# Adding pairs of gated squares on VectorE ahead of the channel sums in a hybrid SSD and latent attention layer, with a new issue order

## The chip, the cores and the metric

The kernel runs on one core of a Trainium2 chip. The metric is the device time of one execution in microseconds. The kernel before takes 652.14 us, the median of 3 runs (651.75 to 652.39).

A core has a matrix engine (TensorE, PE), a vector engine (VectorE, DVE), an activation engine (ScalarE, ACT), a general one (GpSimd, POOL) and a queue engine that here only starts transfers (SyncE, SP). Each runs its own list of instructions in order and waits for the others by semaphores. SBUF is the on-chip memory, 128 partitions wide; PSUM holds what PE accumulates.

## The reference

One layer of an encoder, for 512 new frames and 64 frames of a running stream (576 tokens, width 1024). The input is normalised and projected once; half of the result goes through a state space scan (SSD), half through latent attention (MLA); both are concatenated, projected back, and a SwiGLU feed-forward layer follows.

```
h = rmsnorm(x, norm_mix);  proj = h @ w_in
xbc, conv_new = causal_conv(xbc, ...)                 # silu(conv), width 4
y, h_new = ssd_scan(xh, dt, A, B, C, h0)              # chunks
y = y + d_skip * xh
y = y * silu(z)                                       # the gate
y_ssd = rmsnorm(y, ssd_norm)                          # over 512 channels
... q, k, v; scores; softmax; values -> o
x = x + concat([y_ssd, o]) @ w_out
x = x + (silu(hf @ w_gate) * (hf @ w_up)) @ w_down,   hf = rmsnorm(x)
```

The change is in the sums that the norm of y_ssd needs: for each token, the sum of the squares of the 512 gated channels.

## The kernel before

Everything is kept with channels on partitions and tokens along the free dimension. A row of 1024 channels is 8 tiles of 128 x 576, 512 channels are 4 such tiles. Weights are split in a high and a low part (ACT line 112 copies the high part, DVE line 113 subtracts it), and most products are three PE passes over these parts, in two halves of 288 tokens.

The stages follow each other roughly like this. Up to 20 us: x and the first weights are loaded, and `ps_first` (line 128) makes the latent and query projections; sums of squares go through `ps_norm` (line 162), a product with a matrix of ones that both sums over partitions and copies the sum to all of them. 20 to 90 us: eight `conv_tile` steps (line 376), each a product `ps_in`, its evacuation to `up` (lines 383 to 385, DVE), one tap on ACT (line 390), three on DVE (line 392, tile `cacc`), a tanh on ACT (line 394). Among them stand the rope of the keys (line 301) and the step sizes of the scan (`dt`, `sp_a`, lines 339 to 354). 90 to 155 us: the scan in chunks of 128 tokens (0 to 3) and one of 64 (chunk 4, the running stream), by five steps: `chunk_a` (line 465; transposes `ps_x`, `ps_b`), `chunk_e` (line 501; decays E, products xw and E on DVE, lines 512 and 517), `chunk_b` (line 525; `ps_y`, skip at line 535, `ps_i`, lines 542 and 543), `chunk_s` (line 545; state product `ps_s`, states `h_c`, lines 557 and 558; h_0 is copied by ACT at line 554), and `gate` (line 565). The gate factors sz come from `z_tile` (lines 456 to 460).

`gate(c)` multiplies the chunk by sz (line 570, DVE, in place in xsd), squares it (line 572, ACT, tile ysq), sums the squares over the 512 channels by four products with ones, one for each 128 channels, into the bank ps_g (line 575), and copies the sum to its tokens of a row (line 576, ACT). `norm_y` turns this row into 1/rms, Ry (lines 171 to 178), `cat_tile` multiplies xsd by gain and Ry (line 752, four times) and splits it (lines 142 and 144) into `cat_y0` to `cat_y3`.

From about 145 us attention runs beside that: scores `sc` (line 660, and 666 for the stream), row maxima on DVE (line 643), exponentials on ACT (line 644), scaling (lines 645 to 650), transposes `ptp` (lines 682 and 690), values `pv`. `ps_o` (line 446) multiplies cat_y and the attention output by w_out, and DVE adds it to x (line 738). From about 225 us to the end the feed-forward layer runs (lines 855 and 956).

In what order an engine issues its work is written out by hand: `ISSUE` holds for each of the engines PE, DVE, ACT, POOL and SP a list of instruction numbers, in the order of emission, and `issue_in_order` binds each to the one before it in the list. Numbers that no list names are placed by the framework's scheduler. The steps are emitted in the orders `ORDER_CONV`, `ORDER_SSD`, `ORDER_ATT` and `ORDER_FFN`, which are the same in both kernels.

Of the kernel before, what the change touches and what calls it, by code (L numbers as in the profile page):

```python
# [14 lines left out]
ALU = mybir.AluOpType  # L15
# [39 lines left out]
def hybrid_layer_kernel(ctx: ExitStack, tc: tile.TileContext, a, o):  # L55
    nc = tc.nc
    pe, act, dve, pool, sp = nc.tensor, nc.scalar, nc.vector, nc.gpsimd, nc.sync
# [22 lines left out]
    def tmp(name, w=T):  # L80
        return tpool.tile([P, UPW], F32, tag="t", name=name)[:, :w]
# [10 lines left out]
    ones = cst.tile([P, P], F32, name="ones")  # L92
# [343 lines left out]
    def bank(tag, name):  # L436
        return (psq if tag == "sc" else psh).tile([P, 512], F32, tag=tag, name=name, bufs={"sc": 3, "pp": 3, "hm": 2}[tag])
# [128 lines left out]
    def gate(c):  # L566
        L = P if c < 4 else TS
        tk = slice(c * P, c * P + L)
        yv = xsd[:, :, tk]
        dve.tensor_tensor(yv, yv, sz[:, :, tk], ALU.mult)  # L570
        q = tmp(f"ysq{c}", 4 * L).rearrange("p (t l) -> p t l", t=4)
        act.activation(q, yv, AF.Square)
        ps = bank("pp", f"ps_g{c}")[:, :L]
        for t in range(4):
            pe.matmul(ps, ones, q[:, t], start=t == 0, stop=t == 3)
        act.copy(ssy[:, tk], ps)


# [456 lines left out]
    ps = [lbank(tag, f"ps_l0_{t}", 0) for t, tag in enumerate(("hm", "hm", "sc", "pp"))]  # L1035
# [112 lines left out]

ISSUE = {
    "PE": """  # L1150
0-7 20 14-15 8-10 21-25 11 16-19 32-43 56 12-13 26-31 44-49 62 50-55 68-73 57-61 74-79 92 63-67 80-85 98-100 93-97 110
86-91 104-109 122-127 142-143 134-135 101-103 116-121 136-141 144-147 111-115 128-133 148-171 174 270-274 175 222-229
176-179 172-173 180-221 230-269 275-370 373-420 371 421-468 372 469-590 613-636 591-612 637 641-644 638-640 657-660
665-712 661-664 713-736 645-656 737-760 763-766 771-818 767-770 761-762 819-826 859-861 833-836 862-864 837-840
827-828 831 865 829-830 866-867 832 868-870 880-883 841 845-852 871-873 853-856 842-844 874-879 884-887 857-858
904-909 888-891 910-912 892-900 925-926 913-915 901-903 927-934 916-921 935 939-940 922 936-938 923-924 949-951 964
952-963 965 941 966 945-948 967-970 942-944 971-979 987 980-983 988 984-986 989 991-993 1003 1015-1019 1004-1014
1020-1026 1029-1034 1043-1045 990 994-995 997-1002 1046-1048 996 1049-1054 1027 1035-1042 1028 1059-1064 1075-1076
1055-1056 1081-1092 1057 1077-1080 1058 1093-1104 1065 1121-1123 1066-1067 1071-1072 1068 1105 1124-1127 1069-1070
1128-1132 1108-1110 1073-1074 1133-1144 1106-1107 1119 1145-1156 1229-1237 1120 1238-1240 1111-1112 1115-1118  # L1160
1113-1114 1159-1161 1241-1252 1157 1253-1261 1158 1265-1268 1262-1264 1176 1269-1276 1177-1179 1162-1175 1277
1180-1183 1289 1278-1281 1290-1293 1184-1188 1282-1283 1189 1205-1206 1190-1195 1284-1287 1227 1196-1201 1288 1228
1202-1204 1207-1222 1294-1298 1223-1226 1299-1323 1342-1343 1348-1355 1344-1347 1324-1341 1356-1475 1572 1476-1504
1573 1575 1505-1511 1578 1581-1582 1512-1535 1584 1583 1536-1547 1579 1602 1548-1564 1580 1599-1600 1587-1589 1574
1593 1576 1565-1571 1585-1586 1605-1607 1626-1628 1577 1596 1608 1601 1620 1603-1604 1609-1610 1629 1590-1592
1611-1613 1621-1622 1647 1641 1594-1595 1614-1616 1635-1637 1623-1624 1632 1625 1648-1649 1644 1642-1643 1597-1598
1617-1619 1638 1633-1634 1653-1655 1639-1640 1656 1645-1646 1630 1658-1664 1631 1650-1652 1665-1669 1657 1682
1694-1703 1683-1689 1704-1705 1690-1693 1670-1681 1730-1736 1706-1717 1737-1741 1718-1729 1742-1763 1766 1764-1765
1778-1789 1767-1768 1790-1800 1769-1777 1802-1825 1850-1851 1801 1862-1873 1826-1849 1852-1861 1886-1909 1874-1885
1922-1934 1946-1957 1910-1921 1958-1969 1935-1945 1970-1989 2006-2013 1990-2005 2014-2034 2042-2053 2035-2041  # L1170
2054-2065 2078-2091 2093-2106 2066-2077 2107 2092 2108-2117 2123-2137 2118-2122 2138
""",
    "DVE": """
48 1 0 2-4 7 5-6 10 9 8 11-12 14 13 15-17 20 19 18 23 21-22 30 49 24-25 58 26-28 85 29 31-34 67 36 35 68 108 105 37
106 38 107 109 39 44 94 110 40 69 41 50-51 42 70 52 43 112 121 71 53 72 54 82 55 59-61 130 47 73 56 74 62 75 63 76 64
86-88 77-78 65 79 66 89-90 80 91 57 81 83 95-97 84 46 98-100 113-115 93 92 103 116-117 104 118 122 111 102 139 123 120
119 124 101 45 125-127 131-133 148 155 134-135 128 136 140-142 149 152 138 170 143 150 129 144 153 145 151 154 157 147
156 178 174 146 137 171 159-161 172 162 187 163 175 158 206 164 167 165 169 176 166 183 180 168 181 188 182 177 173
189 215 190 179 195 191-194 184 197 196 224 185-186 204 207 198-201 210 202 208 203 214 209 288 205 211 225 212-213
216-219 222 220 226-229 233 223 230 234 231-232 221 235-236 245 237 246 294 255 247-248 256 239 259 257 260 238  # L1180
263-264 258 261 240 262 241 267 265 242 266 270 243 271 244 268 249 274 251 269 253 250 252 254 275 278 289 277 290
276 272 295 279 287 286 280 282 307 273 297 283 317 291 281 298 296 299 284 318 292 302 285 316 293 319 306 309 303
300-301 312 310-311 313 326-327 304 362 308 328 322 305 320 363 367 323 329 364 321 330 324 336 331-332 325 337 314
366 315 340 333 365 341 377 334-335 344-345 338 346 352 347 339 348-349 342 350 353 351 359 358 343 360 354 356 361
355 357 370 368 371 369 372-373 376 375 374 390 382 378 384 379 383 385 389 386 380 397 387-388 381 405 393 391 395
394 403 392 420 396 401 398 402 462 400 404 406 399 408-409 407 410 463 416-417 464 411 418 412 414 421 469 419 422
413 423-425 428 426 415 427 431-432 438 429 433-435 430 436 439 437 440 442 441 443 466 444 465 446 451 467-468
452-453 455 454 473 447 445 474 470 475 477 448 476 456 472 457 478 449 458 480 482 479 471 488 490-492 481 489 450
493 503 485 504 487 459 505 495 494 507 506 460 500 508 496 486 461 497 518 520 510-511 483 502 521 509 560 522 515
484 519 517 540 523 543 558 524 538 498 526 537 501 512 527 516 513 563 525 528 514 530 499 529 532 542 565 547 555  # L1190
552 573 545 557 570 533 562 539 548 577 568 579 550 534 541 531 580 575 553 544 535 578 546
""",
    "ACT": """
0-5 8 6-7 11 10 9 12-16 18 17 21 20 24 19 23 22 40 25-27 44 51 28-31 50 32 55 33-35 37 36 48 59 41 49 63 38 42 39 67
43 45-47 52-54 56-57 71 58 60-62 64 75 65-66 76 68-70 91 72-74 93 78 89 79 84-85 82-83 80 102 86 88 81 87 100 115 98
96 77 90 103 97 95 99 92 101 125 104 155 109 108 94 111 114 112 110 113 106 116 107 162 141 121 105 117 139 138 118
126 123 134 127 136 119 135 137 120 133 140 128 142 122 129-130 151 144 148 124 209 131 146 132 153 143 147 145 150
149 154 157-158 152 156 159 211 160-161 163-164 169-171 165 167 172 179-180 168 185 173 186 174 188-189 175 166 191
176 192 177 187 178 181 194 193 190 199 195-196 182-184 198 207 200-201 212 214-215 226 202 216 218 208 204 217 233
197 205 210 213 219 203 232 220 206 222 225 227 239-240 228 223 241-243 270 221 230 224 229 236 234 271 235 237 277  # L1200
244 250 245 247 238 231 246 253 249 248 251 256 254 257-258 252 260 263 261-262 283 255 268 267 259 269 265 264 266
272-274 276 275 279-281 284 286 282 292 285 278 290 301 288 287 289 291 293-294 296 299 328-329 297 295 300 302-303
298 305 308 304 309 311 306-307 310 315 312-313 316 314 317 330 318 331 321 319-320 322-324 332 335 334 336 333 337
339 338 325 344 342 345-346 343 347-348 353 326 354 340 355 352 351 327 357 356 362 360 341 363-364 361 366 349 365
373 369 350 374 358 367 370 359 368
""",
    "POOL": """
0-3 7 18 28 4 8 5 9 6 10 26-27 11 29 12-17 20-22 19 23-25 31 30 32-42 53 55 57 59 54 56 58 60 43-52 61-73
""",
    "SP": """  # L1210
11-14 16 15 18 17 19-20 22 21 25 24 23 26 37 33 32 40-41 34 38 42-45 39 46-48 81 57 64 60 79 56 59 65 58 61-62 70 83
63 74 78 67-69 71-72 80 73 66 75 88-89 76-77 82 86 90 87 91-93 100 103 101-102 104-105
""",
}

# [98 lines left out]
```

## Time and profile before

| what | value |
|---|---|
| median of 3 runs | 652.14 us (651.75 to 652.39) |
| profiled execution, its own time | 652.35 us |
| its span | 650.6 us |
| granted TensorE clock | 1.00 |
| PE busy | 640.7 us, 98% |
| weight loads (PEld) busy | 613.4 us, 94% |
| DVE busy | 511.5 us, 79% |
| ACT busy | 338.3 us, 52% |
| POOL busy | 44.3 us, 7% |
| sums of the gate, line 575 | 40 records, 5.7 us of PE |

Busy times overlap, since the engines run beside each other. An fp32 product leaves two records on PE, so the twenty products of the gate are 40. Ends of matmuls are modelled, so PE can look busy where it waits; the weight loads (PEld) stand beside it as a second reading. In a list of waits each row names the waiting engine and tile, what released it, and the total, the number and the longest of the waits. In a timeline the bracket at the end of a row is the idle time ahead of it.

### The profile page before, as it was taken

What the parts mean: (1) busy time and instruction counts of PE and PEld (TensorE: products, weight loads), DVE (VectorE), ACT (ScalarE), POOL (GpSimd) and SP (SyncE); (2) the same over time, 40 slices, a digit from 0 to 9 for tenths busy, and PEclk for the clock granted to TensorE, in tenths of its full rate; (3) what the DMA queues carried; (4) which work ended last, traced back from release to release, by engine and by line L of the source; (5) the groups of instructions that cost most, each with busy time, mean ns of one, the idle gap of its engine ahead of it and who ended that gap; (6) DMA issues with size and microseconds to landing.
All of it is one profiled execution on the core that took longest, in us unless ns stands there. A gap on an engine that the chain in (4) does not pass through costs nothing.

```text
span 650.6 us, 11910 instructions
## 1 busy us (share of the span) xinstructions
PE 640.7 (98%) x4747; PEld 613.4 (94%) x4747; DVE 511.5 (79%) x932; ACT 338.3 (52%) x629; POOL 44.3 (7%) x79
## 2 busy tenths in 40 slices
PE   9999999998999999999999999999999999999996
PEld 9899999885897899999999999999999999999995
DVE  6998996799866699998996776866767776866555
ACT  7654345769676477564523545224533354335364
POOL 1330312001010000000000000000000000000022
PEclk9999999999999999999999999999999999999999
DMA  9620174315020222133322133212323223231004
GB/s 318 219 68 28 39 227 122 111 30 216 33 75 32 99 97 98 44 120 102 126 98 94 69 102 113 79 65 70 94 98 114 81 82 98 82 130 66 1 0 147
DMA packets 26151, 63.22 MB, mean 97 GB/s; under 512 B 3418, under 2 KB 10088, under 8 KB 25840
## 3 DMA queue, kind: packets, MB, share of 16 engines
q1 hardware_dynamic: 24560, 60.77, 27.7%
q0 software_dynamic: 816, 1.13, 0.8%
q8 instruction: 37, 0.61, 0.3%
q10 hardware_dynamic: 720, 0.57, 0.3%
q14 instruction: 18, 0.15, 0.1%
HBM read 58.03 MB, written 3.30 MB: 94 GB/s over the span
## 4 chain that ended last, share of the span: by engine, by line
PE 92%; DVE 4%; ACT 1%; issue 1%; POOL 1%; POOLq 0%; DVEq 0%; ACTq 0%
PE ps_x L855 21%; PE ps_d L956 18%; PE ps_z L855 10%; PE ps_o L446 8%; PE ps_in L128 7%; PE ps_y L855 5%; PE ps_z L446 4%; PE ps_l L956 3%; PE ps_first L128 2%; PE sc L660 2%; PE ps_p L855 2%; PE pv L707 1%; PE ptp L682 1%; PE ps_q L446 1%; PE ps_v L593 1%
## 5 line engine op out<-in xcount | busy, mean ns | idle before, releaser
L956 PE MATMUL ps_d<-pr,wh_d 128*128 128x288 f32 x576 | 115.4, 294 | 0.0
L855 PE MATMUL ps_x<-xop,wh_gu_S 128*128 128x288 f32 x504 | 102.0, 295 | 0.0
L956 PEld LDWEIGHTS ps_d<-pr,wh_d 128*128 128x128 f32 x576 | 92.5, 188 | 0.0
L956 PE MATMUL ps_d<-pr,wl_d 128*128 128x288 f32 x288 | 84.7, 295 | 0.0
L855 PEld LDWEIGHTS ps_x<-xop,wh_gu_S 128*128 128x128 f32 x504 | 80.9, 188 | 0.1
L855 PE MATMUL ps_x<-xop,wl_gu_S 128*128 128x288 f32 x252 | 74.2, 295 | 0.0
L112 ACT CAST wh_gu_S<-gu 128x1024 fp32r<-128x1024 f32 x44 | 46.2, 1050 | 37.4 <-PE ps_d L956 18.5
L113 DVE TENSOR_TENSOR wl_gu_S<-gu,wh_gu_S 128x1024 fp32r<-128x1024 f32 x44 | 53.6, 1222 | 8.3 <-PE ps_d L956 6.6
L956 PEld LDWEIGHTS ps_d<-pr,wl_d 128*128 128x128 f32 x288 | 54.0, 188 | 0.0
L112 ACT CAST wh_d<-wr_d 128x640 fp32r<-128x640 f32 (+1 forms) x32 | 21.5, 674 | 51.0 <-PE ps_x L855 20.4
L855 PEld LDWEIGHTS ps_x<-xop,wl_gu_S 128*128 128x128 f32 x252 | 47.2, 188 | 0.0
L128 PE MATMUL ps_in<-xs,wh_in 128*128 128x288 f32 x256 | 45.5, 299 | 1.0 <-DVE sp_a L351 1.0
L128 PEld LDWEIGHTS ps_in<-xs,wh_in 128*128 128x128 f32 x256 | 37.7, 189 | 1.5 <-ACT up L382 1.2
L855 PE MATMUL ps_z<-xop,gu_a 128*128 128x288 f32 x252 | 37.7, 294 | 0.0
L855 PE MATMUL ps_y<-xop,wh_gu_A 128*128 128x288 f32 x168 | 35.3, 295 | 0.0
L855 PE MATMUL ps_z<-xop,wh_gu_S 128*128 128x288 f32 x168 | 35.3, 297 | 0.0
L855 PEld LDWEIGHTS ps_z<-xop,gu_a 128*128 128x128 f32 x252 | 34.9, 188 | 0.0
L855 PE MATMUL ps_x<-xop,wh_gu_A 128*128 128x288 f32 x168 | 34.5, 296 | 0.0
L113 DVE TENSOR_TENSOR wl_d<-wr_d,wh_d 128x640 fp32r<-128x640 f32 (+1 forms) x32 | 24.2, 756 | 12.5 <-PE ps_x L855 8.1
L112 ACT CAST wh_gu_A<-gu 128x1024 fp32r<-128x1024 f32 x22 | 23.1, 1051 | 19.7 <-PE ps_x L855 12.1
L113 DVE TENSOR_TENSOR wl_gu_A<-gu,wh_gu_A 128x1024 fp32r<-128x1024 f32 x22 | 26.9, 1225 | 8.1 <-PE ps_d L956 4.8
L1052 POOL TENSOR_TENSOR fz<-fz,sq 128x320 f32<-128x320 f32 x3 | 2.7, 886 | 445.8 <-ACT sq L1047 445.8
(337 smaller groups left out, 1652.4 us busy)
## 6 DMA issues: line engine op xcount, KB each, us to landing
gu<-in_w_gu SPq DMA_DIRECT2D x44, 512.0 KB, 3.7
wr_d<-in_w_down SPq DMA_DIRECT2D x16, 320.0 KB, 2.9
wr_in<-in_w_in SPq DMA_DIRECT2D x8, 512.0 KB, 4.4
wr_out<-in_w_out SPq DMA_DIRECT2D x8, 512.0 KB, 3.3
wr_d<-in_w_down SPq DMA_DIRECT2D x16, 256.0 KB, 2.6
cumb<-cumD SPq DMA_DIRECT2D x5, 512.0 KB, 5.8
x<-in_xT SPq DMA_DIRECT2D x2, 1152.0 KB, 5.8
wr_z<-in_w_in SPq DMA_DIRECT2D x4, 512.0 KB, 4.0
```

The source lines that it names most:

```text
L112: act.copy(hi, raw)
L113: dve.tensor_tensor(lo, raw, hi.bitcast(F32), ALU.subtract)
L128: pe.matmul(ps[:m, hf, :n], w, x[:, hf * n : (hf + 1) * n], start=start and k == 0 and i == 0, stop=stop and k == last and i == 2,)
L446: pe.matmul(ps[:, :n], w, x[:, cols], start=k == 0 and i == 0, stop=k == len(terms) - 1 and i == 2,)
L593: pe.matmul(ps[:n], l, r, start=j == 0, stop=j == 2)
L660: pe.matmul(s[:, :nk], qs[:, j, q0 : q0 + P], ks[:, j, :nk], start=True, stop=True)
L682: pe.transpose(pp[:, k : k + P], prs[p, i][:, j, b * P : b * P + P], ident)
L707: pe.matmul(pv[64 * j : 64 * j + 64, b * P :], V[b][:, h * HD : (h + 1) * HD], pts[p, b, j], start=b == 0, stop=True, skip_group_check=b > 0,)
L855: pe.matmul(ps, p, q, start=not onto and first and kp == kps[0] and j == 0, stop=onto or (last and kp == kps[-1] and j == 2), skip_group_c ...
L956: pe.matmul(ps, w, x[:, cols], start=first and k == 0 and i == 0, stop=last and k == len(terms) - 1 and i == 2,)
L1052: pool.tensor_tensor(ss3[:, parts[0]], ss3[:, parts[0]], z, ALU.add)
```

## The change

In `gate`, behind the square, DVE adds the squares of channel tiles 2 and 3 to those of tiles 0 and 1, in place, and PE sums two tiles in place of four. That is one more DVE instruction for each chunk (128 x 256 elements for chunks 0 to 3, 128 x 128 for chunk 4) and ten products fewer.

```diff
         q = tmp(f"ysq{c}", 4 * L).rearrange("p (t l) -> p t l", t=4)
         act.activation(q, yv, AF.Square)
+        dve.tensor_tensor(q[:, :2], q[:, :2], q[:, 2:], ALU.add)
         ps = bank("pp", f"ps_g{c}")[:, :L]
-        for t in range(4):
-            pe.matmul(ps, ones, q[:, t], start=t == 0, stop=t == 3)
+        for t in range(2):
+            pe.matmul(ps, ones, q[:, t], start=t == 0, stop=t == 1)
         act.copy(ssy[:, tk], ps)
...
 ISSUE = {
     "PE": """
-0-7 20 14-15 8-10 21-25 11 16-19 32-43 56 12-13 26-31 44-49 62 50-55 68-73 57-61 74-79 92 63-67 80-85 98-100 93-97 110
...
+0-7 20-21 8 14-17 9-12 22-25 18-19 32-37 13 26-30 38-43 56-58 50-55 68 31 44-49 62-66 59-61 74-79 67 80-85 92-98 69-73
...
```

Lines from 573 on are one higher in the changed kernel. The lists of PE, DVE, ACT and SP are new throughout; the list of POOL is the same. All other instructions are the same in both kernels; where the lists differ, they differ in order only. What moves, read against the names of the instructions:

- SP: the load of hist, and those of the conv weights w_in3, w_in6, w_in0 and w_in2, are issued earlier among the first loads; w_first7, the small weights, cos_sin and ident later.
- PE: the second ps_norm (for the queries) stood behind the first products of ps_in3 and ps_in6; now it stands behind 36 of the products of ps_in6 as well. The two products of ps_s0 are issued together; before, ps_v2 and ps_g4 stood between them. Score products sc1_2_1 and sc1_1_0 stood ahead of the first ps_o with a low part of cat_y0; now they stand behind it. The products ps_q1 moved behind the scores sc0_3.
- DVE: the evacuation of up0 is issued ahead of the scaling of cqn1 and of two of the sp_a steps. The adds of chunks 4 and 0 stand ahead of h_1; the one of chunk 1 behind h_1's second half; those of chunks 3 and 2 between the maxima of sc0_3_0 and sc0_3_1. xw3 stands behind the first two skips (line 535) of chunk 2, and the weight split of pair1 ahead of the last sz. The scaling of pr_0_4 stands ahead of the gains of line 752; the split of cat_y0 ahead of the fourth gain; the maximum of sc1_3_1 behind the split of cat_y3.
- ACT: the square of chunk 4 stands right behind the table load of line 623, two places earlier than before.
- The last part is the same: PE from the first product of the second down stage with pr3 on (328.1 us in the profile before), DVE from 328.2 us, ACT from 318.4 us.

More of the change, by code (lines that the diff above doesn't have):

```diff
@@ L1156 @@
[L1156 to L1160, printed above, removed]
@@ new lines @@
+471 470 449 456 451 472-473 457-458 452 459-460 474 478 461 482 479-480 477 481 462 453-454 475 483-484 476 463 493
+495 486 485 497 494 487 450 455 496 508 490 510 498 492 464 499 501 515 465 512 466 511 500 509 505 513 550 545 516
+491 507 514 502 488 523 525 506 524 520 548 517 543 526 521 565 522 527 560 530 489 575 503 528 531 529 518 532-533
+519 504 542 537 563 534 538 547 552 557 553 562 578 567 582 544 568 535 570 573 584 555 539 546 536 572 585 580 558
+549 554 540 583 551 556 577 559 593 561 589 594-595 564 586 596 566
@@ L1206 @@
+264 266 269 272-274 276 275 283 279 278 280 284 281 292 286 285 287 290 289 282 288 301 291 293 295 294 296 299 297
+300 302 298 303 305 308 304 328 306 309 311 310 307 312 315 313 316 314 329 317 330 318-319 331 320 335 321-324 332
+334 336 333 337 339 338 344 342 345 343 346-347 353 325 348 354 326 351 327 340 352 355 357 356 349 341 360-365 373
+366 358 350 369 367 370 359 368 374-379 371 380
 """,
```

92 lines of the change are left out of this document (45 added, 47 removed).

## The prediction

> **What bounds the kernel now.** I read the page's first and fourth parts, then a table of stages, then the waits of PE, and last the timeline of VectorE (DVE) where the change sits.
>
> ```profile
> PE 640.7 (98%) x4747; PEld 613.4 (94%) x4747; DVE 511.5 (79%) x932; ACT 338.3 (52%) x629; POOL 44.3 (7%) x79
> ...
> PE 92%; DVE 4%; ACT 1%; issue 1%; POOL 1%; POOLq 0%; DVEq 0%; ACTq 0%
> ```
>
> TensorE (PE) carries 92% of the chain that ended last, DVE 4%. That says where the span goes, not what the edited stretch is worth. The stages (columns: us, then busy time and count of PE, weight loads, DVE, ACT, POOL; clock, DMA share, GB/s):
>
> ```profile
> 20.00:60.00 40.00, 38.97 (x281) 35.26 (x279) 37.14 (x64) 21.54 (x32) 12.29 (x19) 1.00 0.31 90
> ...
> 120.00:163.00 43.00, 41.24 (x277) 32.30 (x276) 40.23 (x88) 36.34 (x96) 4.31 (x6) 1.00 0.35 123
> 163.00:225.00 62.00, 62.00 (x452) 50.36 (x451) 43.05 (x106) 39.48 (x106) 2.13 (x4) 1.00 0.16 53
> 225.00:650.60 425.60, 419.89 (x3163) 418.09 (x3161) 326.79 (x554) 199.17 (x314) 8.69 (x11) 1.00 0.26 88
> ```
>
> PE's busy time hides short waits, since ends of matmuls are modelled; the weight loads do not hide them. They fill 418 of 425.6 us after 225, but only 32.3 of 43 us in 120 to 163 and 50.4 of 62 us in 163 to 225. So PE has gaps before 225 and practically none behind. Whatever the change gives or takes is decided by when PE gets through the last gap, near 224; the rest is a rigid tail, whose order of instructions is moreover unchanged from the second down stage (328 us) on. The gates sit in 120 to 163, where DVE is busy 40.2 of 43 us.
>
> ```profile
> 149.82 0.70 DVE mx L643
> ...
> 159.06 2.24 DVE xsd L752 x3
> 161.30 0.31 DVE pr L650
> 161.65 0.52 PE ptp_s L690 x3
> 162.17 0.43 PE sc L660 x2
> ...
> 162.94 0.78 PE ps_o L446 x5
> ```
>
> The chain runs through PE up to 149.8, then through DVE's maxima and the gains of L752, and returns to PE at 161.7 and 162.9. DVE's arrival at the split of cat_y0 therefore sets when PE can start ps_o.
>
> **The change, part by part.**
>
> *Matmuls removed.* Ten of twenty sums, each two records:
>
> ```profile
> L575 PE MATMUL ps_g<-ysq,ones x40: 218/275/275, 125.3 to 154.0; 128*128 128x128 f32 x32, 128*128 128x64 f32 x8
> ...
> 131.99 0.67 PE ps_g L575 x6
> ...
> 136.37 0.89 PE ps_g L575 x8
> ```
>
> By pace a record is 0.89/8 = 0.111 us (0.67/6 agrees). Twenty go: 16 wide ones are 1.78 us; with the 4 narrow ones between half and full price, 2.0 to 2.2. It is PE time in a stretch where DVE ends last, so I count nothing for it in the sum; it only keeps PE ahead of DVE there. If DVE did not end last, it would be worth its 2.1 us.
>
> *Adds put in.* Five on DVE, four of 256 elements per partition and one of 128. No such add is in the trace; the nearest are products of two SBUF tiles of the same size:
>
> ```profile
> 114.99 0.42 DVE L543 TENSOR_TENSOR xsd<-xsd,ecp 128x256 f32<-128x256 f32 x1
> 115.32 0.68 DVE L517 TENSOR_TENSOR E<-E,ps_b 128x512 f32<-128x512 f32 x1
> ...
> 122.50 0.42 DVE L570 TENSOR_TENSOR xsd<-xsd,sz 128x256 f32<-128x256 f32 x1
> 122.84 0.60 DVE L535 SCALAR_TENSOR_TENSOR xsd<-xsd,par,ps_y 128x128 f32<-128x128 f32 x2
> ```
>
> Length 0.42 us, start to next start 0.33 and 0.34. In an engine that is full, the pace counts: 4 x 0.335 + 0.2 (estimate for the half-size one) = 1.54 us; by lengths 4 x 0.42 + 0.3 = 1.98. I take 1.54. [...]
>
> The square on ACT must now be followed by the add before PE starts. For chunk 4 the new ACT order issues the square right behind the table load, two places earlier; for chunks 3 and 2 the adds stand between two maxima. What queues behind an add on DVE is the next row maximum or decay product, and PE's scores and ACT's exponentials wait for those.
>
> *DVE's waits in this stretch.*
>
> ```profile
> DVE h L557 <- ACT h L554: 1.1, 1, 1.1
> ...
> DVE xsd L535 <- PE ps_y L530: 0.5, 1, 0.5
> DVE xw L512 <- ACT E L509: 0.4, 1, 0.4
> DVE sz L460 <- ACT zt L459: 0.3, 1, 0.3
> ```
>
> Together 2.3 us. In the new order: the pair1 weight split comes ahead of the last sz, filling the 0.3; the adds of chunks 4 and 0 come ahead of h_1, and PE issues the two products of ps_s0 together (before, ps_v2 and ps_g4 stand between them), so h_0's copy on ACT and with it h_1 come sooner: the 1.1 goes; ps_y1 follows h_1 as before, but PE is ahead by the matmuls saved: the 0.5 goes; xw3, which waited for E3, now stands behind two skips of chunk 2: the 0.4 goes. I take all 2.3; bounds are 0 (each wait is merely late by what DVE gains) and 2.3.
>
> *Start.*
>
> ```profile
> PE ps_in L128 <- DVE sp_a L351: 1.0, 1, 1.0
> ...
> PE ps_norm L162 <- DVE ssq L154: 0.4, 1, 0.4
> ```
>
> The second ps_norm now stands behind 36 products of ps_in6, so its 0.4 goes. The 1.0 ends with up0's evacuation. The new order clears cqn1's scaling and two sp_a steps from ahead of it, but the row below shows the three conv steps in between waiting on ACT:
>
> ```profile
> 56.84 0.82 DVE L392 SCALAR_TENSOR_TENSOR cacc<-up,hcw,cacc 128x579 f32<-128x579 f32 x1 [0.25 <-ACT cacc L390]
> 57.58 0.20 DVE L351 SCALAR_TENSOR_TENSOR sp_a<-sp_a,sp_q 128x40 f32<-128x40 f32 x1
> 57.70 0.82 DVE L392 SCALAR_TENSOR_TENSOR cacc<-up,hcw,cacc 128x579 f32<-128x579 f32 x1
> ```
>
> ACT's table load and cacc come in the same order as before, so this wait stays. I take 0.4; bounds 0 and 1.4. SP issues its first loads in another order: hist and two weight tiles earlier; w_first7, the small weights, cos_sin and ident later.
>
> ```profile
> 4.85 15.56 PE ps_first L128 x108
> ...
> wr_in<-in_w_in SPq DMA_DIRECT2D x7, 512.0 KB, 4.9
> ...
> GB/s 318 219 68 28 39 227 122 111 30 216 33 75 32 99 97 98 44 120 102 126 98 94 69 102 113 79 65 70 94 98 114 81 82 98 82 130 66 1 0 147
> ```
>
> I cost this at nothing, because the chain shows ps_first running through for 15.6 us with no load in it, so the last w_first tiles came ahead of their use. If that cover is too short, w_first7 is late by at most the one 512 KB load now ahead of it: at the 318 GB/s of the first slice an estimated 1.6 us.
>
> *From the first maximum to cat_y0.* Old order:
>
> ```profile
> 148.59 0.68 DVE L643 TENSOR_REDUCE mx<-sc 128x1 f32<-128x512 f32 x1
> ...
> 157.94 0.68 DVE L643 TENSOR_REDUCE mx<-sc 128x1 f32<-128x512 f32 x1
> ...
> 161.51 0.81 DVE L752 SCALAR_TENSOR_TENSOR xsd<-xsd,par,Ry 128x576 f32<-128x576 f32 x1
> 162.24 2.09 DVE L144 TENSOR_TENSOR cat_y<-xsd,cat_y 128x576 fp32r<-128x576 f32 x3
> ```
>
> The new order puts the maximum of sc1_3_1 (0.68) and the fourth L752 (0.81) behind cat_y0's split, and two adds (0.67) ahead: -0.82.
>
> *Sum.* DVE reaches the first maximum at -0.4 - 2.3 + 0.87 (adds 4, 0 and 1) = -1.8 us, and cat_y0's split at -1.8 - 0.8 = -2.6, near 159.6 in place of 162.24. But PE gets there with more left to do: two score products (sc1_2_1 and sc1_1_0, 384 and 256 columns; the 256 one is the chain's 0.43, so 0.65 + 0.43) are moved behind: +1.0. Net -1.6 us. All five adds are in this sum, three ahead of the first maximum and two behind it.
>
> From there to 224 both programs have the same pieces in another order. I count 0 for that and bounds of 1.5 us on either side: a little more than one weight split, the longest DVE step that moved:
>
> ```profile
> L113 DVE TENSOR_TENSOR wl_gu_S<-gu,wh_gu_S 128x1024 fp32r<-128x1024 f32 x44 | 53.6, 1222 | 8.3 <-PE ps_d L956 6.6
> ```
>
> Behind 225 PE is full, so moves there cost nothing, unless DVE's evacuations come late. The profiled execution took 652.35 us, 0.21 above the median 652.14; against the median: 652.14 - 1.6 = **650.5 us**.
>
> **The rivals.** 0.2% is 1.3 us, about what a measurement of this kernel can tell from no change; so "same" is 650.8 to 653.4.
>
> *No change to tell.* The removed matmuls lie beside DVE, worth nothing; of the 2.3 us of waits half stay, because they end on ACT and PE, not on DVE: -0.4 - 1.15 + 0.87 - 0.8 + 1.0 = -0.5, 651.6. For it: ACT is busy 36.3 of 43 us there. Against: h_1's releaser is visibly brought forward.
>
> *Larger gain.* PE is what ends last after all once DVE is ahead: 2.1 of matmuls, 1.4 at the start, and 163 to 225 loses some of its 11.6 us without weight loads, say one step of 0.7: 652.14 - 4.2 + 1.0 = 648.9. For it: that slack is large, and each earlier row maximum starts a softmax earlier. Against: the score products moved behind fill the same place.
>
> *Slower.* One mechanism: the adds go wholly onto DVE's chain in 120 to 163, none of its waits is filled, and ps_o starts late: +1.54 to +1.98, 653.7 to 654.1. It decides once less than about 0.5 of the 2.3 us is absorbed and the re-sorted maxima wait on scores that PE now issues later. For it: 93% of that stretch is DVE busy. Against: the L752 gains no longer have sc1_3_1 ahead of them, and DVE idles in 163 to 225 for 19 of 62 us.
>
> **How the numbers follow.** Forecast 0.35 (its own range 649.4 to 651.5, the part above 650.8 given to "same"), larger gain 0.20, no change 0.25, slower 0.20. So faster 0.55, same 0.25, slower 0.20. The range reaches down past the larger gain (648.9) to 648.4, not to the sum of all lower bounds, and up to 653.7, where the slower case begins.
>
> **What would show it.** Right: sums of L575 fall to 20 records and 2.8 us; five new adds near 0.42 us; the four DVE waits listed gone or under 0.3 each; ps_norm no longer waits; cat_y0's first split near 159.6; weight loads in 163 to 225 short by the same 11.6 or so; everything after 328 us shifted whole by -1.6. Wrong: a new wait of DVE for ACT's squares or for PE's scores, PE waiting for an evacuation in 60 to 90, a split of cat_y0 after 161, or new gaps in 163 to 225, where I have worked out nothing but the bounds.

## The result, and the profile after

The changed kernel takes 653.24 us, the median of 15 runs (652.39 to 655.61). The kernel before takes 652.24 us beside it (651.75 to 652.59, 15 runs). The ratio is 1.0021, with an interval from 1.0012 to 1.0029: slower by about 0.2%, 1.00 us between the medians. The forecast was 650.5 us and faster; the time lies near the upper end of the range. It also lies in the band that the prediction called no change (650.8 to 653.4), but the interval of the ratio leaves no change out.

The profiled execution of the changed kernel took 655.61 us with a span of 653.8 us. It is the longest of the 15, 2.4 us above the median, so a part of what its trace shows is not in a usual run. The page's first part and the stages (columns: us, then busy time and count of PE, weight loads, DVE, ACT, POOL; clock, DMA share, GB/s):

```profile
PE 641.5 (98%) x4727; PEld 612.9 (94%) x4727; DVE 514.4 (79%) x937; ACT 338.4 (52%) x629; POOL 41.6 (6%) x79
```

```profile
20.00:60.00 40.00, 39.25 (x287) 35.98 (x286) 37.84 (x66) 21.32 (x33) 12.56 (x21) 1.00 0.33 96
...
120.00:163.00 43.00, 38.67 (x242) 29.52 (x243) 39.50 (x88) 34.34 (x90) 4.37 (x6) 0.96 0.36 127
163.00:225.00 62.00, 62.00 (x444) 49.38 (x443) 42.80 (x106) 40.67 (x110) 2.21 (x4) 1.00 0.12 39
225.00:650.60 425.60, 422.74 (x3180) 420.71 (x3178) 328.57 (x557) 200.10 (x315) 8.68 (x11) 1.00 0.28 89
```

The start has gained: 36.0 us of weight loads lie in 20 to 60, 35.3 before. In 120 to 163 the weight loads fall from 32.3 to 29.5 us and from 276 to 243. Twenty of those are the ten removed products; the other 13 run behind 163, because they are late or because the new order has them later. The granted clock is 0.96 in this stretch, 1.00 before. The waits of PE in the whole run (columns: who waited, for whom, us in total, times, longest) name the place, and those of DVE in 118 to 165 name what lies behind it:

```profile
PE ps_g L576 <- DVE ysq L573: 2.5, 2, 2.0
...
PE ps_in L128 <- DVE up L385: 0.4, 1, 0.4
...
PE ps_in L128 <- DVE sp_a L351: 0.3, 1, 0.3
PE ps_p L856 <- DVE xop L804: 0.3, 1, 0.3
```

```profile
DVE wl_pair L113 <- ACT wh_pair L112: 1.8, 1, 1.8
DVE zh L456 <- PE ps_z L446: 0.9, 1, 0.9
DVE h L557 <- ACT h L554: 0.9, 1, 0.9
DVE xsd L535 <- PE ps_y L530: 0.4, 1, 0.4
DVE h L558 <- PE ps_s L551: 0.3, 1, 0.3
```

A wait of PE for an add, 2.0 us, and a wait of DVE for the high part of the pair1 weights, 1.8 us, were not there before. Of the four waits of DVE that the prediction let go, the one for h_0's copy (1.1) is still 0.9 and the one for ps_y (0.5) is 0.4. The five rows come to 4.3 us; the kernel before has 3.1 in the same list (the prediction's four and 0.8 for ps_z). In place of 2.3 us less there are 1.2 more. The timelines of the three engines show how the two new waits hang together. ACT first, then DVE, then PE, all of the changed kernel:

```profile
120.23 0.63 ACT L510 ACTIVATE ecp<-ecp 128x512 f32<-128x512 f32 x1 [3.80 <-DMA ecp<-cumD]
...
121.06 0.50 ACT L112 CAST wh_pair<-wr_pair 128x384 fp32r<-128x384 f32 x1
121.46 0.68 ACT L459 ACTIVATE zt<-zh 128x576 f32<-128x576 f32 x1
```

```profile
121.59 0.56 DVE L113 TENSOR_TENSOR wl_pair<-wr_pair,wh_pair 128x384 fp32r<-128x384 f32 x1 [1.81 <-ACT wh_pair L112]
122.17 0.76 DVE L460 SCALAR_TENSOR_TENSOR sz<-zt,zh 128x576 f32<-128x576 f32 x1
...
125.71 0.28 DVE L573 TENSOR_TENSOR ysq<-ysq 128x128 f32<-128x128 f32 x1
...
163.00 0.75 DVE L144 TENSOR_TENSOR cat_y<-xsd,cat_y 128x576 fp32r<-128x576 f32 x1
```

```profile
126.05 0.66 PE L576 MATMUL ps_g<-ysq,ones 128*128 128x64 f32 x4 [1.99 <-DVE ysq L573]
```

ACT waits 3.8 us for a load of ecp2, whose exponential (line 510) stands first in its new order. The conversion of pair1's high part and zt3 stand behind it, and so does all that DVE wants next: the pair1 split waits 1.8 us, then come sz3, the gate of chunk 4, the state h_4, four skips and the add of chunk 4. PE's list has ps_g4 right behind the four transposes ps_x2, so PE stands for 2.0 us. The first split of cat_y0 comes at 163.00, not at the forecast 159.6.

The kernel before issues the last loads of ecp no earlier (116.70 us, against 115.51) and pays nothing for them, because its ACT does the exponential after what DVE needs, and its DVE asks for pair1 four microseconds later. Its SP, ACT and DVE timelines (SP's rows give start and length of the issue):

```profile
108.75 0.55 SPq L476 DMA_DIRECT2D cumb<-cumD  x1
...
116.70 1.17 SPq L482 DMA_DIRECT2D ecp<-cumD  x1
```

```profile
121.40 0.50 ACT L112 CAST wh_pair<-wr_pair 128x384 fp32r<-128x384 f32 x1
121.80 0.62 ACT L510 ACTIVATE ecp<-ecp 128x512 f32<-128x512 f32 x1
```

```profile
121.23 0.76 DVE L460 SCALAR_TENSOR_TENSOR sz<-zt,zh 128x576 f32<-128x576 f32 x1 [0.28 <-ACT zt L459]
...
125.68 0.55 DVE L113 TENSOR_TENSOR wl_pair<-wr_pair,wh_pair 128x384 fp32r<-128x384 f32 x1
```

### The profile page after: what moved, and what is told of

It reads as the page before. It is cut to its first block, busy times and chain, and to the rows that moved or that the text cites. A ratio compares the mean times of both kernels' runs of the same rounds, so it can differ in the third digit from the quotient of the medians.

```text
span 653.8 us, 11875 instructions
## 1 busy us (share of the span) xinstructions
PE 641.5 (98%) x4727; PEld 612.9 (94%) x4727; DVE 514.4 (79%) x937; ACT 338.4 (52%) x629; POOL 41.6 (6%) x79
## 4 chain that ended last, share of the span: by engine, by line
PE 69%; DVE 5%; issue 1%; POOL 1%; ACT 0%; POOLq 0%; DVEq 0%; ACTq 0%
PE ps_x L856 21%; PE ps_d L957 18%; PE ps_z L856 10%; PE ps_o L446 5%; PE ps_y L856 5%; PE ps_l L957 3%; PE sc L661 2%; PE pv L708 2%; PE ptp L683 1%; PE ps_p L856 1%; DVE xop L804 1%; DVE x L739 1%; DVE fz L154 1%; PE ps_q L446 0%; PE ps_k L446 0%
## 5 line engine op out<-in xcount | busy, mean ns | idle before, releaser
L856 PE MATMUL ps_y<-xop,wh_gu_A 128*128 128x288 f32 x168 | 35.3, 295 | 0.0
L856 PE MATMUL ps_z<-xop,wh_gu_S 128*128 128x288 f32 x168 | 35.3, 297 | 0.0
L970 DVE TENSOR_TENSOR x<-ps_d,x 128x288 f32<-128x288 f32 x64 | 28.5, 452 | 3.8 <-PE ps_d L957 3.6
```

Source lines behind the costliest of these rows:

```text
L856: pe.matmul(ps, p, q, start=not onto and first and kp == kps[0] and j == 0, stop=onto or (last and kp == kps[-1] and j == 2), skip_group_c ...
L970: dve.tensor_tensor(x2[t][:, cols], ps, x2[t][:, cols], ALU.add)
```

## The experiments

The theory after the two traces: the new order makes the scan wait for a load (ecp2, and cumb2 queued behind it on SP), and the adds and the rest are as priced. Its rivals: the adds themselves are the loss; the early pair1 split alone is; the lost PE clock after the gap is; the late part of the new order is.

Every kernel is given by its median less that of the kernel before, measured beside it ("against before"). The intervals of the ratios are some 0.0009 to either side, 0.6 us, so a difference of under 0.8 us between two kernels needs the traces beside it. All twelve compute the whole layer; f4 repeats four transposes beyond that. A diff line that begins with ISSUE tells in words what the lists are; where the number of products or adds changes, the numbers in the lists change with it, and the diff shows the gate alone.

| kernel | gate | order | median us (lowest to highest, runs) | against before, us | ratio (interval) |
|---|---|---|---|---|---|
| changed kernel | adds | new | 653.24 (652.39 to 655.61, 15) | +1.00 | 1.0021 (1.0012 to 1.0029) |
| e1 | old | new | 654.09 (652.96 to 655.13, 8) | +2.06 | 1.0028 (1.0018 to 1.0038) |
| e2 | adds | old | 653.55 (653.11 to 653.84, 11) | +1.52 | 1.0020 (1.0011 to 1.0029) |
| e3 | adds | new, ecp2's exponential later | 652.64 (651.64 to 654.17, 11) | +0.61 | 1.0007 (0.9998 to 1.0016) |
| e4 | adds | new, pair1 split later | 653.61 (653.16 to 654.08, 10) | +1.58 | 1.0022 (1.0013 to 1.0031) |
| f1 | old | new up to 88 us, then old | 651.41 (651.02 to 651.84, 11) | -0.64 | 0.9989 (0.9980 to 0.9998) |
| f2 | adds | new up to 163 us, then old | 655.30 (653.45 to 655.71, 5) | +3.25 | 1.0041 (1.0029 to 1.0054) |
| f3 | adds | e3, cumb2's load earlier | 651.38 (651.13 to 652.49, 11) | -0.67 | 0.9992 (0.9983 to 1.0001) |
| f4 | adds | new, 16 transposes more | 653.43 (652.88 to 655.36, 8) | +1.38 | 1.0024 (1.0013 to 1.0034) |
| g1 | adds | f3 up to 226 us, then old | 650.56 (650.21 to 652.51, 10) | -1.63 | 0.9978 (0.9969 to 0.9988) |
| g2 | old | f3's | 652.46 (652.22 to 653.23, 11) | +0.27 | 1.0007 (0.9998 to 1.0016) |
| g3 | adds on POOL | f1's | 651.73 (651.49 to 652.12, 11) | -0.46 | 0.9993 (0.9985 to 1.0002) |
| g4 | adds | new, cumb2's load earlier | 653.88 (653.24 to 655.55, 5) | +1.69 | 1.0033 (1.0021 to 1.0046) |

Of e4 one execution took 3552 us and is left out. It was the profiled one: in its trace PE leaves 436 records in 330 to 640 us, where the kernel before has 2331, though the granted clock reads 1.00 in both, so there is no trace of e4 to compare.

Where the time goes is read from the start times of the same PE instruction in two traces. The numbers are its start less that in the kernel before (us, worked out from the two traces; a minus is earlier). The start of each column holds some 0.5 us that isn't the change: e2, whose start is the old one, stands at -0.53 too. The kernels with the new start also differ there by 0.9 among themselves (-0.67 to -1.60). So a column is read by its steps from row to row.

| PE instruction (time before) | changed | e1 | e2 | e3 | f1 | f3 | g1 | g2 | g3 |
|---|---|---|---|---|---|---|---|---|---|
| last of ps_in4 (66.5) | -0.67 | -1.53 | -0.53 | -1.60 | -1.42 | -1.37 | -1.29 | -1.53 | -1.49 |
| ps_v1 (124.1) | -1.14 | -2.01 | -0.53 | -2.09 | -1.42 | -1.84 | -1.76 | -2.01 | -1.50 |
| ps_y3 (141.3) | +1.32 | -1.44 | +0.09 | -1.61 | -1.42 | -3.20 | -3.13 | -2.11 | -0.97 |
| ps_o0_0 (165.3) | +1.66 | -0.95 | +0.98 | +0.25 | -1.40 | -2.87 | -2.79 | -1.51 | -0.96 |
| ps_o0_6 (223.3) | +2.29 | -0.30 | +0.99 | +0.86 | -1.40 | -2.26 | -2.12 | -0.84 | -0.96 |
| second down stage (329.5) | +3.12 | +0.49 | +0.99 | +1.66 | -1.32 | -1.48 | -2.04 | -0.06 | -0.94 |
| last down stage (640.0) | +3.14 | +0.50 | +0.99 | +1.68 | -1.32 | -1.09 | -1.67 | -0.05 | -0.94 |

**e1: the orders alone.** The new order with the old gate.

```diff
-        dve.tensor_tensor(q[:, :2], q[:, :2], q[:, 2:], ALU.add)
         ps = bank("pp", f"ps_g{c}")[:, :L]
-        for t in range(2):
-            pe.matmul(ps, ones, q[:, t], start=t == 0, stop=t == 1)
+        for t in range(4):
+            pe.matmul(ps, ones, q[:, t], start=t == 0, stop=t == 3)
```

> The new issue order with the old gate: four products a chunk, no add. Chain theory (in the changed kernel ACT's exponential of ecp2 waits 3.8 us for its load, so the split of pair1 and DVE behind it come 1.8 us late, PE idles 2.0 us at ps_g4 and runs at half its clock for 3.3 us after): the wait of DVE for wh_pair stays near 1.8, PE's wait at ps_g4 shrinks by the add and the steps ahead of it to about 1 us; 652.4 to 653.4, slower than before. Theory that the adds cost it (1.5 to 2.0 us on a full DVE): faster than before, near 651.5.

The time is 2.06 us above before, more than with the adds and more than either range that was expected. So the adds are not what makes the changed kernel slow: in this order they give back 1.06, by intervals that overlap in part (g2 and f3 show 0.94 in a mended order). The wait for pair1 is there without them:

```profile
DVE wl_pair L113 <- ACT wh_pair L112: 1.4, 1, 1.4
```

The profile of e1 (652.96 us) is that of its shortest run, so its column in the table looks better than its median. All eight runs have a mean granted clock of 0.998 or more, so what e1 loses is not the clock.

**e2: the adds alone.** The old order with the new gate. The adds stand behind the old neighbours: chunk 4 behind its xdt2, chunk 0 behind E1's second product, chunk 1 behind the split of wl_out0_0, chunks 3 and 2 behind the maximum of sc0_3_1.

```diff
-ISSUE: the new lists
+ISSUE: the old lists; in DVE's the five adds, in PE's two products a chunk for four
```

> The old issue order with the adds put in behind xdt2, behind chunk 1's decay product, behind the first out weight split, and two behind the maximum of sc0_3_1; two products a chunk. Chain theory: the adds fall partly into DVE's waits and PE's saving makes up for the rest, 651.5 to 652.8, no change to tell, clock 1.00 from 124 to 133. Theory that the adds cost it: 653.6 to 654.1.

1.52 us above before, where the theory had 651.5 to 652.8 us and is refuted for the adds in the old order. The trace loses it in two steps: 0.6 between ps_v1 and ps_y3, 0.9 more by ps_o0_0, nothing later. PE waits for the adds here as well:

```profile
PE ps_g L576 <- DVE ysq L573: 2.5, 3, 1.1
```

This is the price of the prediction's slower rival (1.54 to 1.98) in the place where it was put. Together with e1 it makes a square: old order and old gate 0, adds alone +1.52, order alone +2.06, both +1.00. The two don't add up: they are worth 2.58 us less than their sum. Each alone costs; the adds pay only where the order is built for them.

**e3: ecp2's exponential back behind zt3.** In ACT's list of the changed kernel number 141 goes three places on; nothing else moves.

```diff
-115 90 99-100 102 97 88 104 96 101 112 109 98 125 108 110 94 107 155 106 114 113 141 111 162 116 105 121 117-118 140
+115 90 99-100 102 97 88 104 96 101 112 109 98 125 108 110 94 107 155 106 114 113 111 162 116 141 105 121 117-118 140
```

> The changed kernel with one ACT instruction moved back: the exponential of ecp2 stands behind zt3 again. Chain theory: ACT's wait of 3.8 us for the load of ecp2 no longer holds wh_pair1 and zt3, DVE's wait for wh_pair1 falls from 1.8 to under 0.5, PE's gap at ps_g4 falls under 1 us and the clock does not drop; 650.3 to 651.8. Theory that the adds or the later stages cost it: as the changed kernel, 653.2.

+0.61 against the changed kernel's +1.00, with overlapping intervals, so the time alone decides little; it is above the 650.3 to 651.8 us that were expected. The profile (654.17 us, the longest of its runs) tells more: the wait for pair1 is gone, and a new one stands a few instructions later, on ACT and from there on DVE (waits of DVE, then ACT's timeline):

```profile
DVE ysq L573 <- ACT ysq L572: 1.8, 1, 1.8
```

```profile
122.21 0.21 ACT L478 ACTIVATE el<-cumb 128x8 f32<-128x8 f32 x1 [1.68 <-DMA cumb<-cumD]
```

ACT now waits for cumb2 instead of ecp2. Both are loaded from cumD, and SP issues cumb2 behind ecp2. A mended wait turned into the next one on the same queue.

**e4: the pair1 split back.** In DVE's list of the changed kernel number 227 goes back to its old neighbour, ahead of E1's product.

```diff
-188 182 218 183 189 227 190 195 179 191-194 196 198 197 184 199 185-186 206 209 200-205 212 216 210 207 217 211 293
+188 182 218 183 189-190 195 179 191-194 196 198 197 184 199 227 185-186 206 209 200-205 212 216 210 207 217 211 293
```

> The changed kernel with one DVE instruction moved back: the split of pair1 stands behind xdt2 and the first add again, not ahead of sz3. Chain theory: sz3 then waits for ACT's zt3, which still stands behind the load of ecp2, so about half of the 1.8 us stays as a wait of sz for zt; 651.5 to 652.8. If the late split itself was the whole cause: 650.5 to 651.2. Theory of the adds: 653.2.

No gain, +1.58. So the place of the split is not the whole cause. The split shows the wait, and sz3 behind it wants zt3, which stands behind the same exponential on ACT; this is argued from the lists, since no trace of e4 shows it.

**f1: the start alone.** The kernel before, with the new order for everything that starts ahead of 88 us there.

```diff
-ISSUE: the old lists
+ISSUE: the new lists for what starts before 88 us, the old ones for the rest
```

> The kernel before (four products, no add), with the new issue order only for what it did in its first 88 us (up to the end of the convolution); the rest in the old order. If the start's two waits of PE (ps_norm 0.4 and ps_in4 1.0) are what the new order gains: 0.7 to 1.4 us faster than before, 650.8 to 651.5, and a lead in the trace that stays constant to the end. If the lead is lost again in the part bound by DVE (120 to 163 us): as before, 652.0.

0.64 us faster than before, an interval (0.9980 to 0.9998) that leaves out no change; in the trace the lead is constant behind the start. The term of 0.4 was right in kind and a little small.

**f2: the late order back.** The changed kernel with the old order from 163 us on.

```diff
-ISSUE: the new lists
+ISSUE: the new lists for what starts before 163 us, the old ones for the rest
```

> The changed kernel (two products, adds) with the old issue order for everything that the kernel before did after 163 us; before that, the new order. If the new order of the attention and of the first feed-forward tiles costs about 0.6 us in 165 to 223 and 0.8 us in 238 to 329, as the traces say: 1.4 us faster than the changed kernel, 651.5 to 652.2. If those differences only reflect a late start of the stage: as the changed kernel, 653.2.

+3.25, and inconclusive for what it was made for: where the two orders meet, a wait of its own appeared, which neither kernel has (waits of PE):

```profile
PE sc L661 <- ACT pr L645: 2.9, 2, 2.2
```

Behind 176 us its trace loses nothing (+2.91 there, +2.90 at the end), which already points at the late order; g1 puts the joint at a better place.

**f3: cumb2's load ahead of ecp2's as well.** e3, and in SP's list the load of cumb2 (number 71) ahead of those of pair1 and ecp2.

```diff
-67 74 78 68 80 72-73 71 75 66 88 77 76 89 82 87 86 90-93 100 103 101-102 104-105
+67 74 78 68 71 80 72-73 75 66 88 77 76 89 82 87 86 90-93 100 103 101-102 104-105
```

> The changed kernel with ecp2's exponential behind zt3 on ACT (as in the run with it moved back) and, on SP, the load of cumb2 issued ahead of wr_pair1 and ecp2, as in the kernel before. If the queue of SP is the root (cumb2 waits behind ecp2, whose buffer is free only at 115 us, so el2, the table load and the square of chunk 4 come late): ACT's wait for cumb2 (1.7 us) and the add's wait for the square (1.8 us) go, PE's gap at ps_g4 falls under 0.5 us, the clock stays at 1.00 between 124 and 133; 651.0 to 652.2. If the late load is hidden by the adds and the maxima behind it: 652.6, as with ecp2 alone.

-0.67: 1.67 us better than the changed kernel by two moved instructions. The queue of SP, the wait of PE for the adds and DVE's waits in 118 to 165 of f3:

```profile
112.19 0.33 SPq L476 DMA_DIRECT2D cumb<-cumD  x1
...
114.80 2.15 SPq L482 DMA_DIRECT2D ecp<-cumD  x2
```

```profile
PE ps_g L576 <- DVE ysq L573: 0.5, 1, 0.5
```

```profile
DVE zh L456 <- PE ps_z L446: 0.9, 1, 0.9
...
DVE h L558 <- PE ps_s L551: 0.3, 1, 0.3
DVE sz L460 <- ACT zt L459: 0.3, 1, 0.3
```

In the changed kernel SP issues cumb2 at 116.87, behind ecp2 at 115.51, where the kernel before had it at 108.75, ahead:

```profile
115.51 1.24 SPq L482 DMA_DIRECT2D ecp<-cumD  x2
116.87 4.71 SPq L476 DMA_DIRECT2D cumb<-cumD  x2
```

With the loads mended three of the four waits that the prediction let go are gone; the fourth, sz for zt, stays at 0.3. cat_y0's split starts at 158.47:

```profile
158.47 0.75 DVE L144 TENSOR_TENSOR cat_y<-xsd,cat_y 128x576 fp32r<-128x576 f32 x1
```

**f4: fill the gap.** The changed kernel, with the transposes ps_x2 made five times over ahead of ps_g4, to keep PE busy while it waits.

```diff
-        for t in range(4):
+        for t in range(20 if c == 2 else 4):
+            t = t % 4
             pe.transpose(px[:L, t * P : t * P + P], xsd[:, t, tk], ident)
```

> The changed kernel with the four transposes of ps_x2 repeated four times ahead of ps_g4 (16 more products of 128 columns, about 1.8 us, writing the same values): PE is busy in the 2.0 us in which it waited for the first add. If the idle time is what takes the clock to 0.50 for 3.3 us: the clock stays at 1.00 in 124 to 133, and the time falls by up to 1.6 us, 651.8 to 652.8, with less spread. If the clock drops for another reason, or its drop hides under DVE: 653.2 and the same spread, up to 655.

+1.38, no gain. In its profile the wait of PE for the adds is 0.5 and the clock is 1.00 from 118 to 133; it falls to 0.50 at another place instead (two of its windows of 3 us):

```profile
127.00:130.00 3.00, 3.00 (x28) 2.17 (x27) 3.00 (x7) 2.62 (x9) 0.00 (x0) 1.00 0.00 0
...
157.00:160.00 3.00, 3.00 (x9) 1.81 (x9) 3.00 (x8) 2.78 (x7) 0.82 (x2) 0.50 0.36 99
```

Since this trace loses the clock elsewhere for as long (156.7 to 160.1 us), f4 doesn't show what that loss is worth. The mean granted clock of each run says more. Of the changed kernel's 15 runs, five have 0.997 or more and took 652.39 to 653.00 us (median 652.72); ten have 0.996 or less and took 652.60 to 655.61 (653.65). So with its clock kept the changed kernel is still some 0.5 us slower than before, and an estimated 0.5 of its +1.00 goes with the clock.

**g4: cumb2's load alone.** The changed kernel with f3's list for SP and its own for ACT.

```diff
-67 74 78 68 80 72-73 71 75 66 88 77 76 89 82 87 86 90-93 100 103 101-102 104-105
+67 74 78 68 71 80 72-73 75 66 88 77 76 89 82 87 86 90-93 100 103 101-102 104-105
```

> The changed kernel with one SP instruction moved: the load of cumb2 ahead of wr_pair1 and ecp2, ACT's order left as it is. If the place of that load is the root by itself: 651.2 to 652, the table load no longer waits for el2. If ecp2's exponential ahead of zt3 is needed for the loss as well, wh_pair1 still waits for ecp2's load on ACT and DVE for it about 1.5 us: 652.5 to 653.3.

+1.69, no help: ACT still waits for ecp2 with pair1 behind it (ACT's timeline); DVE waits 1.3 us for pair1, against 1.8 in the changed kernel.

```profile
119.49 0.63 ACT L510 ACTIVATE ecp<-ecp 128x512 f32<-128x512 f32 x1 [3.24 <-DMA ecp<-cumD]
```

Each half alone gives nothing that the times can tell from the changed kernel (e3 0.39 better, g4 0.69 worse); both together give 1.67.

**g1: the old order at the end.** f3, with the old order for everything that starts behind 226 us in the kernel before, where nothing but the feed-forward layer is left to join.

```diff
-ISSUE: the lists of f3
+ISSUE: the lists of f3 for what starts before 226 us, the old ones for the rest
```

> The run with cumb2 first (651.4), with the old issue order for everything that the kernel before did after 226 us. If the new order loses 0.8 us between 238 and 329, where the prediction had counted nothing: 650.4 to 650.9, and a lead that stays constant from 238 on. If that loss is only a difference in order that is paid either way: 651.4.

650.56 us, 0.22% faster than before (0.9978, 0.9969 to 0.9988) and 0.43% below the changed kernel by the quotient of the two ratios: it beats both. The step from f3 is 0.96 us between kernels that were not measured beside each other, with intervals that just overlap. The traces carry it: from ps_o0_6 to the second down stage every kernel in the table with the new order loses 0.8 us (changed 0.83, e1 0.79, e3 0.80, f3 0.78, g2 0.78), and every one with the old order at most 0.1 (e2 0.00, f1 0.08, g1 0.08, g3 0.02). Between f3 and g1 that is 0.7. A part of it, 0.3, is a wait of PE in the first products of the feed-forward layer. It stands in the changed kernel's waits above and in f3, and g1 has none; weight loads in 250 to 255, first f3, then g1:

```profile
250.00:255.00 5.00, 4.70 (x37) 4.47 (x35) 5.00 (x12) 3.10 (x6) 0.00 (x0) 1.00 0.00 0
```

```profile
250.00:255.00 5.00, 5.00 (x40) 5.00 (x39) 5.00 (x12) 3.55 (x7) 0.00 (x0) 1.00 0.12 34
```

DVE is busy for all 5 us in both. What differs is when it reaches the operand xop (line 804) that ps_p wants. What takes the rest of the 0.8 is not shown.

**g2: f3 without the adds.** f3's lists and the old gate; the diff of the gate is that of e1.

```diff
-        dve.tensor_tensor(q[:, :2], q[:, :2], q[:, 2:], ALU.add)
...
+        for t in range(4):
+            pe.matmul(ps, ones, q[:, t], start=t == 0, stop=t == 3)
```

> The run with cumb2 first, but with the old gate (four products, no add) in the same mended order. If the adds cost DVE 1.5 us net in any order, as they do in the old one: 649.9 to 650.5. If the mended order has room for them, so that the change of the gate itself is worth nothing or a little: 651.2 to 652.

+0.27 against f3's -0.67, and above both ranges that were expected: with the loads mended, adds and fewer products together are worth 0.94 us, next to 1.06 in the unmended order (changed kernel against e1). In the traces f3 leads g2 by 1.1 at ps_y3 and by 1.4 at ps_o0_0; between the two g2's trace has 3.4 us at half the clock (from 155.7 us on), f3's none. How much of that is the ten products and how much the place of the square's sum in PE's list was not taken apart: both orders were made for two products.

**g3: the adds on POOL.** f1's order with the new gate, the add moved to the general engine.

```diff
-        dve.tensor_tensor(q[:, :2], q[:, :2], q[:, 2:], ALU.add)
+        pool.tensor_tensor(q[:, :2], q[:, :2], q[:, 2:], ALU.add)
```

> The start's new order, the old order from 88 us on, two products a chunk, and the five adds on POOL in place of DVE (POOL is nearly idle there). The same with the adds on DVE would be near 652.9 (653.55 less the 0.64 that the start gained). If the adds cost by DVE's time: 651.0 to 651.6, as the start alone. If they cost because PE waits for one more step between square and sum: 652.5 to 653.5, for a POOL add is no quicker.

-0.46, which is f1's -0.64 within the intervals. On DVE the adds cost 1.5 in the old order, on POOL 0.2 or nothing, although a single add takes up to 3.3 times as long (1389 ns, next to the median of 416 on DVE) and PE waits for it (the form of the line, and the waits of PE):

```profile
L573 POOL TENSOR_TENSOR ysq<-ysq x5: 456/726/1389, 123.7 to 148.7; 128x256 f32<-128x256 f32 x4, 128x128 f32<-128x128 f32 x1
```

```profile
PE ps_g L576 <- POOL ysq L573: 1.4, 2, 1.1
```

So in the old order it is mainly DVE's time that the adds cost, not the one more step between square and sum. That step and the ten products fewer come to nothing there together; what each is worth alone was not taken apart.

## Why the prediction was wrong

**The step that failed** is that of DVE's waits: "the pair1 weight split comes ahead of the last sz, filling the 0.3", and "I take all 2.3". The list of moves was read for DVE and PE. On ACT it was read for one square only, on SP for the first loads only. The moves of ecp2's exponential ahead of pair1's conversion and zt3, and of cumb2's load behind ecp2's, are not among the moves listed. In place of a wait of 0.3 there is one of 1.8, and PE has one of 2.0 for the add of chunk 4. Mending the two places (f3) is worth 1.67 us; an estimated 0.5 of that goes with the clock (see f4). The rows of the kernel before held a warning: pair1's high part is ready there at 121.90 (121.40 and 0.50), while DVE starts sz at 121.23. A split put ahead of that sz could not fill 0.3 us; it had to wait for some 1.0, unless ACT's work moved as well.

**The second step that failed** is "Behind 225 PE is full, so moves there cost nothing, unless DVE's evacuations come late". The condition holds in kind: an operand of DVE comes late for 0.3 us, and 0.8 us go in all (0.7 between the traces of f3 and g1, 0.96 by their times). That the late order costs is shown; which waits make up all of it is not.

In number the two account for the miss: forecast -1.6, measured +1.00, difference 2.6; the loads 1.67 and the late order 0.96 make 2.63. So close a fit is luck, for each step is known to some 0.8 us only. That g1, with both mended, stands at -1.63 is in part luck too, since within it other terms are off in both directions, as follows.

- *Start, 0.4.* Right in kind, and small: 0.64 in f1. ps_norm's wait is gone as said. The 1.0 of ps_in4 did not stay; it is 0.3 in the changed kernel, and at 52.7 us there is a new wait of 0.4 for an evacuation (up, line 385). The three together, 0.7 us less, agree with f1. SP's first loads cost nothing that the traces show: the last product of ps_first starts at 25.2 to 26.0 us with the new order of loads, at 25.8 and 25.3 with the old (before, e2).
- *Length of the adds.* Right: 278 ns for the short one, a median of 416 for all five, and 0.33 us from one start to the next (127.72 to 128.05), so the pace lies below the length here as well. The row of the line in the changed kernel:

```profile
L573 DVE TENSOR_TENSOR ysq<-ysq x5: 278/416/425, 125.7 to 151.5; 128x256 f32<-128x256 f32 x4, 128x128 f32<-128x128 f32 x1
```
- *Matmuls removed, nothing.* Not contradicted in the old order (g3: with the adds off DVE there is no gain). In the two new orders adds and removed products together gain 1.0 (1.06 and 0.94), so "I count nothing for it in the sum" doesn't hold there. The twenty records are gone as said (x20 for x40).
- *From the first maximum to cat_y0.* The split was to start near 159.6. It starts at 163.00 in the changed kernel and at 158.47 in f3: that part of the order does what was read from it, once what comes before it is on time.
- *163 to 224, nothing, with bounds of 1.5.* It costs 0.6 to 0.7 in every kernel of the table that has the new order there (changed 0.63, e1 0.65, e3 0.61, f3 0.61, g1 0.67, g2 0.67), and 0.01 in e2, 0.00 in f1 and g3. Within the bounds, but not nothing. Weight loads fall short of the stage by 12.6 us where 11.6 was said. Which wait takes it was not taken apart.
- *Everything behind 328 us shifted whole.* Right: +3.12 and +3.14 in the changed kernel's trace. It does not hold for f3 and g1, which lose 0.4 more there, at a wait of PE (ps_n, from 631 us on) for DVE's fz that is 0.5 and 0.4.
- *Rivals.* The slower one was right in its price and its mechanism for the adds in the old order (e2), but that is not why the changed kernel is slower; the adds help there. None of the rivals had a new wait on a load. Of the signs of a wrong prediction, none of them with a price, one came true: a split of cat_y0 after 161, at 163.00. The new waits that came were not those named: DVE waits for the high part of pair1, not for ACT's squares or PE's scores, and PE for an add and, at 52.7 us, for an evacuation, not in 60 to 90. The rival of no change had half of the waits stay; that isn't what the traces show either.

## What to carry over

Where an order moves an instruction forward, look up in the trace of before when each of its operands is ready, on every queue that makes it; here a row of ACT and one of the load queue decided that (a wait of 1.8 us), not the idle time of 0.3 us on the engine that it was moved on. Of an order that is new throughout, read the moves on all engines in the stretch that counts, the load queue's too: one load and one exponential, put back, were worth more here (1.67 us) than the edit itself. And try the edit in the old order and the order without the edit: here each alone was slower by 1.5 to 2.1 us, and the gain lay in the pair, with a few instructions put back.

## What the runs showed of the chip that was not expected

In the changed kernel a gap of 1.99 us on PE was followed by 3.4 us at half the granted clock. The windows of 3 us around it:

```profile
124.00:127.00 3.00, 1.01 (x9) 0.95 (x9) 3.00 (x9) 1.66 (x5) 0.00 (x0) 0.96 0.51 153
127.00:130.00 3.00, 3.00 (x11) 2.64 (x11) 2.33 (x5) 2.13 (x7) 0.00 (x0) 0.50 0.32 123
130.00:133.00 3.00, 3.00 (x29) 2.38 (x29) 2.42 (x7) 2.92 (x8) 0.58 (x1) 0.97 0.01 3
```

From the clock column the low stretch lasts 0.24 + 3.00 + 0.18 = 3.4 us at 0.50. The same shows in f2 after a gap of 2.16 us (PE's timeline, then the window):

```profile
164.29 0.70 PE L661 MATMUL sc<-ks,qs 100*128 100x256 f32 x2 [2.16 <-ACT pr L645]
```

```profile
165.00:168.00 3.00, 3.00 (x16) 3.00 (x16) 0.23 (x1) 0.67 (x2) 0.00 (x0) 0.58 0.00 0
```

And e3 has two such stretches on end from 155 us on where PE is only lightly loaded (weight loads fill 0.79 of 3 us in 152 to 155), with no wait above 0.7 us:

```profile
124.00:127.00 3.00, 2.43 (x17) 2.01 (x17) 2.81 (x6) 2.92 (x9) 0.00 (x0) 1.00 0.32 122
152.00:155.00 3.00, 1.86 (x11) 0.79 (x9) 2.94 (x10) 2.91 (x11) 0.00 (x0) 1.00 0.98 414
155.00:158.00 3.00, 3.00 (x4) 1.08 (x5) 2.41 (x10) 2.94 (x10) 1.96 (x4) 0.50 0.82 289
158.00:161.00 3.00, 3.00 (x10) 2.10 (x9) 3.00 (x6) 2.11 (x4) 0.00 (x0) 0.50 0.03 7
```

Its longest wait for an add, 1.4 us, had none behind it (the first row: 1.00):

```profile
PE ps_g L576 <- DVE ysq L573: 1.9, 2, 1.4
```

Whether such a stretch comes differs from run to run. The changed kernel's mean granted clock goes from 0.999 to 0.994 over its 15 runs, and one stretch of 3.4 us at 0.50 takes an estimated 0.0026 off the mean (half of 3.4 us, of a span of 653.8). The traces of f4 and g2 have a stretch in the same place as e3's, from 156.7 and 155.7 us on; f3 and g1 have the same waits of PE ahead of it (0.7 and 0.4) and no stretch. Nor does it always cost: f3's two runs at 0.994 and 0.995 took 651.68 and 651.27 us, about its median of 651.38. What decides whether it comes was not settled.
